# A recurrence whose filling work is handed out anew: one output projection and half of the last values go to the two last scans

## The chip, the cores and the metric

The kernel runs on one core of a Trainium2 chip. The metric is device microseconds (us) of one execution. The kernel before took 1845.09 us, the median of three runs (1844.77 to 1849.04). The profile shows one execution of 1847.34 us, whose span from first to last instruction is 1845.5 us.

## What is computed

Two layers of a diffusion transformer on 512 latent and 256 context tokens of width 1024, in fp32. Layer 0 mixes the tokens by attention, layer 1 by a gated linear recurrence in both directions (HGRN2, 8 heads of 128 key and 128 value channels). Each layer ends in a SwiGLU feed-forward block. Of layer 1 only the latent tokens are needed behind the mixer. The part that the change touches, cut from the reference:

```python
def hgrn2_mixer(h_lat, h_ctx, w_in, lb, out_norm, w_o, with_ctx_out):
    def gates(z):
        f = lb + (1.0 - lb) * jax.nn.sigmoid(z.astype(jnp.float32))
        return heads(jnp.log(f)), heads(1.0 - f)
    ...
    s_fw = hgrn2_final_state(kc_fw, gc_fw, vc)            # context tokens
    s_bw = hgrn2_final_state(flip(kc_bw), flip(gc_bw), flip(vc))
    q, gate = query_gate(h_lat)
    g_fw, k_fw, g_bw, k_bw, v = recurrent_inputs(h_lat)
    o_fw, _ = hgrn2_chunk_scan(q, k_fw, g_fw, v, s_fw)
    o_bw, _ = hgrn2_chunk_scan(flip(q), flip(k_bw), flip(g_bw), flip(v), s_bw)
    return readout(o_fw + flip(o_bw), gate), y_c          # rms_norm, sigmoid gate, @ w_o
```

and then `h = h + gt1 * y` and the feed-forward block.

## The kernel before

Activations lie with channels on the 128 partitions and tokens along the free axis. Each large fp32 product is three products of a high and a low part (`mm3`, lines 112 to 114): weights are loaded into a ring of 1024-column tiles (`load_split`: 4 raw buffers, 3 for the high and 3 for the low parts), ScalarE casts the high part (line 88) and VectorE subtracts it (line 91, "split").

The recurrence runs head by head. One head scan (`scan_head`) is a generator of 14 steps. First VectorE adds the two directions' keys (`kfb`) and TensorE forms the product `A` (line 1548). Then come seven levels: in each, TensorE forms a product `lv` of halves of the chunks (line 1566), ScalarE copies the keys for it (`kc`, 2 buffers), VectorE scales the queries (`QD`, line 1573) and copies `lv` into `A` under a mask (line 1581), and GpSimd scales the keys (`KD`, line 1573). Then the keys are transposed (`ktp`), the states are formed (`pu`, `S`) and the output is read out (`ho`). Behind the readout stands a chain over ScalarE (`osq`), VectorE (`oss`, `on`) and GpSimd (power, and the gating `on*sg`), whose result is transposed (`hot`) in the next scan and scaled into `oth` and `otl`. `kfb` and `osq` share one buffer, and so do the six-column factors `FB` of all heads.

A scan alone leaves TensorE waiting. So the projections are put between its steps as filling work (`Fill.run` with a credit for each step): `head_proj` (products `hq` of 512 columns and `hz` of 512 and 256: query and the two forget gates of a head), `pair_proj` (`hv`, 256 columns: values of two heads), `gate_proj` (`hg`, 256 columns: output gates of two heads) and `wo_pair` (`hwo`, 512 columns: output projection of two heads, with the residual on VectorE, line 676). `head_proj` ends each gate with `FB` and `KD` on GpSimd (lines 1514 and 1515), which the next head's first product needs. The scans 1 to 6 (h = 0 to 5) run one after the other, the two last ones interleaved. Each engine executes in the order in which this code issues. What a scan doesn't use of its fill is drained behind it; the last `wo_pair` goes into the feed-forward block.

Of the kernel before, what the change touches and what calls it, by code (L numbers as in the profile page):

```python
# [16 lines left out]
P = 128  # L17
D = 1024
# [24 lines left out]
TAIL_BUDGET = (8, 1.6)  # L43
# [4 lines left out]
def kernel(  # L48
# [212 lines left out]
    def sumsq_add(acc, sqp, h, k, first, eng=None, tag="sq", bufs=2, width=T):  # L261
        if first:
            ACT.activation(acc, h, AF.Square)
        else:
            sq = sqp.tile([P, width], F32, tag=tag, bufs=bufs, name=f"sq{k}")
            sq = sq[:, : h.shape[1]]
            ACT.activation(sq, h, AF.Square)
            (eng or DVE).tensor_tensor(acc, acc, sq, op=ALU.add)
# [391 lines left out]
    hT = [hpool.tile([P, T], F32, name=f"hT{k}") for k in range(KT)]  # L660

    def residual_in():
# [5 lines left out]
        for k in range(KT):  # L668
# [3 lines left out]
            ACT.copy(hT[k], ps[:, 0:T])  # L672
# [149 lines left out]
    def ffn(layer, only_lat, pre, begin, tail=None):  # L822
# [172 lines left out]
        def fo_out(p_, o, ps, v, a, e):  # L995
            residual(o, ps, layer, 5, v, a, e)
            if p_ == len(parts) - 1:
                sumsq_add(acc_n[:, a:e], late_pool[0], hT[o][:, a:e], o, o == 0, POOL if v else DVE,
                          tag=f"g{8 + (o + v) % 2}", bufs=1, width=n)
# [120 lines left out]
        for h in range(2):  # L1120
            hs = slice(h * H, (h + 1) * H)
            for o in range(KT):
                next(pre)
                sumsq_add(acc_n[:, hs], fp, hT[o][:, hs], o, o == 0, DVE if o % 2 else POOL, tag="sw", bufs=2, width=512)
# [82 lines left out]
    def ffn_plain(layer, only_lat, begin, late, pre=None, tail=None):  # L1207
# [33 lines left out]
        def token_scale():  # L1241
            acc_o = fp.tile([P, T], F32, tag="gl0", name="acc_o")
            for k in range(KT):
                odd = k % 2
                sumsq_add((acc_o if odd else acc_n)[:, :n], fp, hT[k][:, :n], k, k < 2, POOL if odd else DVE)
# [47 lines left out]
        for part, (j0, nj) in enumerate(PARTS[1]):  # L1293
# [50 lines left out]
            def fo_chain(o, w, ps, v, a, e):  # L1344
# [3 lines left out]
                if final:  # L1348
                    sumsq_add(acc_n[:, a:e], fp, hT[o][:, a:e], o, o == 0)
# [106 lines left out]
    def token_proj(c0, ntok, name, evac):  # L1456
        ws = [w_in(c0, 256, 4 * i, 4, f"{name}{i}") for i in range(2)]
        for t in range(ntok):
# [21 lines left out]
    def pair_proj(pr_):  # L1480
        v2 = hnp.tile([P, NT, 256], F32, tag=f"xt2{'hl'[pr_ % 2]}", name="v2")
        sg2 = hp.tile([P, NLT, 256], F32, tag="sg2", bufs=1, name="sg2")
        hv["v", pr_], hv["g", pr_] = v2, sg2
        yield from token_proj(4 * D + pr_ * 256, NT, f"hv{pr_}", lambda t, ps: ACT.copy(v2[:, t], ps))

    def gate_proj(pr_):
        sg2 = hv["g", pr_]
        yield from token_proj(D + pr_ * 256, NLT, f"hg{pr_}",
# [49 lines left out]
    def scan_head(h):  # L1538
# [98 lines left out]
        oth = hop.tile([P, NL], F32R, tag=f"oth{h % 2}", name="oth")  # L1637
        otl = hop.tile([P, NL], F32R, tag=f"otl{h % 2}", name="otl")
# [24 lines left out]
    for h in range(GH - 2):  # L1663
        fill = Fill()
        budget = 20.8
        if h % 2 == 0:
            fill.add(gate_proj(h // 2))
            budget += 10.4
            if h >= 2:
# [95 lines left out]
```

## Time and profile before

| | |
|---|---|
| median of three runs | 1845.09 us |
| profiled execution, its span | 1847.34 us, 1845.5 us |
| attention, first feed-forward block | to about 960 us of the span |
| recurrence (eight scans) | about 970 to 1453 us |
| second feed-forward block | about 1453 to 1845 us |
| TensorE, VectorE, ScalarE, GpSimd busy | 96%, 66%, 42%, 29% of the span |

Times in the rows are microseconds from the span's start. In a timeline a row begins with start and duration, then engine, line, operation, result and inputs; a bracket at the end gives the idle time of that engine just before and what ended it. A row may stand for several instructions (x8). The granted clock is a share of TensorE's full speed, 2.4 GHz.

### The profile page before, as it was taken

To read this page: it belongs to the slowest core of one execution; us is meant where nothing else is said; L and a number is where in the kernel's file an instruction comes from. 1 tells how busy PE (TensorE), PEld (TensorE's weight loads), DVE (VectorE), ACT (ScalarE), POOL (GpSimd) and SP (SyncE) were. 2 spreads that over 40 slices of the span, in tenths; PEclk is the share of its full clock that TensorE was granted. 3 is DMA by queue.
4 is the path that set the end of the run, shared out by engine and by line. 5 is a ranking of instruction groups with operands and counts; after the bars stand their busy time and mean duration, and the time that the engine had idled before them with its cause. 6 is when DMAs were issued, how large, how long until landed. Compare 5 with 4: busy or idle time off the path is not lost.

```text
span 1845.5 us, 30295 instructions
## 1 busy us (share of the span) xinstructions
PE 1780.8 (96%) x11929; PEld 1627.0 (88%) x11929; DVE 1224.5 (66%) x2097; ACT 765.9 (42%) x1465; POOL 543.2 (29%) x508
## 2 busy tenths in 40 slices
PE   8979999999999999999999989999998999999998
PEld 6779688988899989898988889898997899898997
DVE  3586688888878787878756475656738774344443
ACT  4333787777533425252545233333323432222234
POOL 1244255445513314141315264443535100000000
PEclk9999999999999999999999999999999999999999
DMA  9433510002033232525231212112211253333321
GB/s 329 160 115 86 166 59 24 14 11 75 23 111 112 71 119 75 154 87 171 63 109 45 69 58 81 59 57 80 80 52 29 86 166 92 93 89 94 100 85 56
DMA packets 213198, 166.41 MB, mean 90 GB/s; under 512 B 7696, under 2 KB 190144, under 8 KB 213056
## 3 DMA queue, kind: packets, MB, share of 16 engines
q1 hardware_dynamic: 212768, 163.43, 28.7%
q8 instruction: 94, 1.54, 0.3%
q10 hardware_dynamic: 288, 1.05, 0.1%
q14 instruction: 48, 0.39, 0.1%
HBM read 162.36 MB, written 2.10 MB: 89 GB/s over the span
## 4 chain that ended last, share of the span: by engine, by line
PE 83%; DVE 8%; ACT 3%; POOL 3%; issue 2%; DMA 1%; POOLq 0%; SPq 0%; DVEq 0%; ACTq 0%
PE ffo L112 5%; PE ffo L113 5%; PE ffo L114 5%; PE ffi L112 5%; PE ffi L113 5%; PE ffi L114 5%; PE pt L703 3%; PE x L112 2%; PE x L113 2%; PE x L114 2%; PE lv L1566 2%; PE hz L112 2%; PE hz L113 2%; PE hz L114 2%; PE sc L645 2%
## 5 line engine op out<-in xcount | busy, mean ns | idle before, releaser
L112 PE MATMUL ffi<-fnh,whi_fi 128*128 128x256 f32 x704 | 198.9, 283 | 0.1
L113 PE MATMUL ffi<-fnl,whi_fi 128*128 128x256 f32 x704 | 198.0, 281 | 0.9 <-DVE fnl L1236 0.9
L114 PE MATMUL ffi<-fnh,wlo_fi 128*128 128x256 f32 x704 | 197.8, 281 | 0.0
L113 PEld LDWEIGHTS ffi<-fnl,whi_fi 128*128 128x128 f32 x704 | 133.2, 189 | 1.5 <-DVE fnl L1236 1.3
L112 PEld LDWEIGHTS ffi<-fnh,whi_fi 128*128 128x128 f32 x704 | 132.7, 189 | 0.5 <-issue 0.3
L114 PEld LDWEIGHTS ffi<-fnh,wlo_fi 128*128 128x128 f32 x704 | 132.8, 189 | 0.0
L676 DVE SCALAR_TENSOR_TENSOR hT<-ffo,modc,hT 128x512 f32<-128x512 f32 (+1 forms) x106 | 67.0, 636 | 90.8 <-PE ffo L114 90.7
L1573 POOL TENSOR_TENSOR KD<-KD,tot 128x384 f32<-128x384 f32 x96 | 101.5, 1081 | 67.8 <-ACT kc L1556 66.2
L280 POOL TENSOR_TENSOR rc<-rc,mhalf 128x2 f32<-128x2 f32 (+2 forms) x7 | 6.3, 906 | 379.3 <-DVE rc L278 379.3
L693 POOL TENSOR_SCALAR pf<-pf,st 128x768 f32<-128x768 f32 (+1 forms) x96 | 73.6, 769 | 127.9 <-DVE st L692 91.6
L88 ACT CAST whi_fi<-raw_fi 128x1024 fp32r<-128x1024 f32 x44 | 46.2, 1051 | 146.7 <-PE ffi L113 72.7
L114 PE MATMUL ffo<-gh,wlo_w 128*128 128x512 f32 (+1 forms) x304 | 102.6, 338 | 0.0
L113 PE MATMUL ffo<-gl,whi_w 128*128 128x512 f32 (+1 forms) x304 | 102.3, 337 | 0.0
L112 PE MATMUL ffo<-gh,whi_w 128*128 128x512 f32 (+1 forms) x304 | 101.6, 337 | 0.0
L91 DVE TENSOR_TENSOR ptl<-pt,pth 128x384 fp32r<-128x384 f32 (+1 forms) x160 | 79.8, 523 | 12.4 <-ACT pth L88 11.2
L1556 ACT COPY kc<-KD 128x256 f32<-128x256 f32 x112 | 43.0, 414 | 102.7 <-PE lv L1566 37.6
L689 DVE TENSOR_REDUCE st<-sc 128x1 f32<-128x768 f32 (+1 forms) x96 | 74.2, 773 | 15.3 <-PE sc L646 12.5
L88 ACT CAST pth<-pt 128x384 fp32r<-128x384 f32 (+1 forms) x160 | 69.9, 461 | 34.2 <-PE pt L703 22.4
L235 DVE SCALAR_TENSOR_TENSOR adacc<-adw,csil,adacc 128x512 f32<-128x512 f32 x98 | 82.0, 850 | 2.1 <-DMA adw<-in_ada_w_dram 1.8
L1573 DVE TENSOR_TENSOR QD<-QD,tot 128x256 f32<-128x256 f32 x96 | 55.5, 619 | 41.1 <-PE lv L1566 40.4
L691 ACT ACTIVATE pf<-sc,st 128x768 f32<-128x768 f32 (+1 forms) x96 | 73.4, 765 | 19.3 <-DVE st L689 18.4
L703 PE MATMUL pt<-ident,pf 128*128 128x128 f32 x448 | 72.2, 276 | 5.1 <-DVE ptl L91 3.9
(852 smaller groups left out, 5980.6 us busy)
## 6 DMA issues: line engine op xcount, KB each, us to landing
raw_fi<-in_ffn_w_in_dram SPq DMA_DIRECT2D x44, 512.0 KB, 3.7
adw<-in_ada_w_dram SPq DMA_DIRECT2D x40, 512.0 KB, 4.5
adw<-in_ada_w_dram SPq DMA_DIRECT2D x80, 256.0 KB, 3.1
raw_hz<-in_hgrn_w_in_dram SPq DMA_DIRECT2D x14, 512.0 KB, 3.6
raw_fo<-in_ffn_w_out_dram SPq DMA_DIRECT2D x16, 448.0 KB, 3.8
adr<-in_ada_w_dram SPq DMA_DIRECT2D x16, 256.0 KB, 4.7
adr<-in_ada_w_dram SPq DMA_DIRECT2D x8, 512.0 KB, 6.8
raw_wq<-in_attn_w_qkv_dram SPq DMA_DIRECT2D x8, 512.0 KB, 6.2
```

The costliest lines, as they stand in the source:

```text
L88: ACT.copy(hi, src)
L91: (eng or DVE).tensor_tensor(lo, src, hi.bitcast(F32), op=ALU.subtract)
L112: PE.matmul(ps, ahi, bhi, start=first, stop=False, **kw)
L113: PE.matmul(ps, ahi, blo, start=False, stop=False, **kw)
L114: PE.matmul(ps, alo, bhi, start=False, stop=last, **kw)
L235: pin(DVE.scalar_tensor_tensor(a, raw, cc, a, op0=ALU.mult, op1=ALU.add))
L676: DVE.scalar_tensor_tensor(hT[o][:, a:e], ps, mcol(layer, ch, o, v), hT[o][:, a:e], op0=ALU.mult, op1=ALU.add)
L689: DVE.tensor_reduce(st3[:, 0:1], ps[:, :nk], op=ALU.max, axis=AX.X, negate=True)
L691: ACT.activation(pf, ps[:, :nk], AF.Exp, bias=st3[:, 0:1], accum_out=st3[:, 1:2])
L693: POOL.tensor_scalar(pf, pf, st3[:, 2:3], 1.0, op0=ALU.mult, op1=ALU.mult)
L703: PE.transpose(pt[:, i * P : (i + 1) * P], pf[:, (i0 + i) * P : (i0 + i + 1) * P], ident)
L1573: eng.tensor_tensor(view, view, f, op=ALU.mult)
```

## The change

- The fill of the first scan is `head_proj(1)` and then `gate_proj(0)`; it was the other way round.
- `wo_pair(1)` (48 products of 512 columns) leaves the fifth scan (h = 4), the second half of the tokens of `pair_proj(3)` (72 products of 256 columns) leaves the sixth (h = 5); both are filling work of the two last scans now. The halves of `pair_proj` load and split their weights each for itself. The credits of each step are set anew (`TAIL_BUDGET` 1.6 to 2.6).
- The context tokens lie in tiles of their own (`hC`), and two of these are used again for `oth` and `otl` of the heads 2 and 3, which now live longer. Where an operation spanned latent and context tokens, it is issued in two pieces (the copy in `residual_in`, the square in `sumsq_add`).

```diff
--- before.py
+++ after.py
@@ -40,7 +40,7 @@
 Q_LAG = 3
 SOFTMAX_LAG = 3
 PV_LAG = 6
-TAIL_BUDGET = (8, 1.6)
+TAIL_BUDGET = (8, 2.6)
 LEVELS = [1, 2, 4, 8, 16, 32, 64]
 
 
@@ -258,14 +258,14 @@
 
 
 
-    def sumsq_add(acc, sqp, h, k, first, eng=None, tag="sq", bufs=2, width=T):
-        if first:
-            ACT.activation(acc, h, AF.Square)
-        else:
-            sq = sqp.tile([P, width], F32, tag=tag, bufs=bufs, name=f"sq{k}")
-            sq = sq[:, : h.shape[1]]
-            ACT.activation(sq, h, AF.Square)
-            (eng or DVE).tensor_tensor(acc, acc, sq, op=ALU.add)
+    def sumsq_add(acc, sqp, hs, k, first, eng=None, tag="sq", bufs=2, width=T):
+        sq = acc if first else sqp.tile([P, width], F32, tag=tag, bufs=bufs, name=f"sq{k}")
+        at = 0
+        for h in hs:
+            ACT.activation(sq[:, at : at + h.shape[1]], h, AF.Square)
+            at += h.shape[1]
+        if not first:
+            (eng or DVE).tensor_tensor(acc, acc, sq[:, :at], op=ALU.add)
 
     def rstd_cols(pl, acc, n, tag="rc", late=False):
         nt = n // P
@@ -657,7 +657,18 @@
     qes.close()
 
     hpool = pool("hT", side="right")
-    hT = [hpool.tile([P, T], F32, name=f"hT{k}") for k in range(KT)]
+    class Tokens:
+        def __init__(self, lat, ctx_):
+            self.lat, self.ctx = lat, ctx_
+
+        def __getitem__(self, at):
+            a, e = at[1].start, at[1].stop
+            if e <= NL:
+                return self.lat[:, a:e]
+            return self.ctx[:, a - NL : e - NL]
+
+    hC = [hpool.tile([P, 2, NC], F32, tag=f"hC{k}", name=f"hC{k}") for k in range(KT // 2)]
+    hT = [Tokens(hpool.tile([P, NL], F32, name=f"hT{k}"), hC[k // 2][:, k % 2]) for k in range(KT)]
 
     def residual_in():
         for k in range(KT):
@@ -669,7 +680,8 @@
             ps = s2(f"rx{k}")
             for t in range(NT):
                 PE.transpose(ps[:, t * P : (t + 1) * P], hT[k][:, t * P : (t + 1) * P], ident)
-            ACT.copy(hT[k], ps[:, 0:T])
+            ACT.copy(hT[k][:, 0:NL], ps[:, 0:NL])
+            ACT.copy(hT[k][:, NL:T], ps[:, NL:T])
             yield
 
     def residual(o, ps, layer, ch, v, a, e):
...
@@ -1242,7 +1254,7 @@
             acc_o = fp.tile([P, T], F32, tag="gl0", name="acc_o")
             for k in range(KT):
                 odd = k % 2
-                sumsq_add((acc_o if odd else acc_n)[:, :n], fp, hT[k][:, :n], k, k < 2, POOL if odd else DVE)
+                sumsq_add((acc_o if odd else acc_n)[:, :n], fp, [hT[k][:, :n]], k, k < 2, POOL if odd else DVE)
             DVE.tensor_tensor(acc_n[:, :n], acc_n[:, :n], acc_o[:, :n], op=ALU.add)
             yield
             rc = rstd_cols(fp, acc_n[:, :n], n)
...
@@ -1453,9 +1465,9 @@
         src = hgrn_w_in[0, k0 * P : (k0 + nk) * P, c0 : c0 + n].rearrange("(k p) n -> p k n", p=P)
         return load_split(src, [P, nk, n], name, eng)
 
-    def token_proj(c0, ntok, name, evac):
+    def token_proj(c0, toks, name, evac):
         ws = [w_in(c0, 256, 4 * i, 4, f"{name}{i}") for i in range(2)]
-        for t in range(ntok):
+        for t in toks:
             ps = s2(name)
             ts_ = slice(t * P, (t + 1) * P)
             for k in range(KT):
@@ -1477,15 +1489,16 @@
 
     hv = {}
 
-    def pair_proj(pr_):
-        v2 = hnp.tile([P, NT, 256], F32, tag=f"xt2{'hl'[pr_ % 2]}", name="v2")
-        sg2 = hp.tile([P, NLT, 256], F32, tag="sg2", bufs=1, name="sg2")
-        hv["v", pr_], hv["g", pr_] = v2, sg2
-        yield from token_proj(4 * D + pr_ * 256, NT, f"hv{pr_}", lambda t, ps: ACT.copy(v2[:, t], ps))
+    def pair_proj(pr_, toks=range(NT)):
+        if toks.start == 0:
+            hv["v", pr_] = hnp.tile([P, NT, 256], F32, tag=f"xt2{'hl'[pr_ % 2]}", name="v2")
+            hv["g", pr_] = hp.tile([P, NLT, 256], F32, tag="sg2", bufs=1, name="sg2")
+        v2 = hv["v", pr_]
+        yield from token_proj(4 * D + pr_ * 256, toks, f"hv{pr_}{toks.start}", lambda t, ps: ACT.copy(v2[:, t], ps))
 
     def gate_proj(pr_):
         sg2 = hv["g", pr_]
-        yield from token_proj(D + pr_ * 256, NLT, f"hg{pr_}",
+        yield from token_proj(D + pr_ * 256, range(NLT), f"hg{pr_}",
                               lambda t, ps: ACT.activation(sg2[:, t], ps, AF.Sigmoid))
 
     def head_proj(h):
@@ -1634,8 +1647,11 @@
         for ck in range(NLT):
             PE.transpose(pt[:, ck * P : (ck + 1) * P], on[:, ck], ident)
         wcol = cols2[:, 32 + h : 33 + h]
-        oth = hop.tile([P, NL], F32R, tag=f"oth{h % 2}", name="oth")
-        otl = hop.tile([P, NL], F32R, tag=f"otl{h % 2}", name="otl")
+        if h in (2, 3):
+            oth, otl = (hpool.tile([P, NL], F32R, tag=f"hC{2 * (h - 2) + i}", name="oth" if i == 0 else "otl") for i in range(2))
+        else:
+            oth = hop.tile([P, NL], F32R, tag=f"oth{h % 2}", name="oth")
+            otl = hop.tile([P, NL], F32R, tag=f"otl{h % 2}", name="otl")
         ACT.activation(oth, pt, AF.Copy, scale=wcol)
         DVE.scalar_tensor_tensor(otl, pt, wcol, oth.bitcast(F32), op0=ALU.mult, op1=ALU.subtract)
         hv["o", h] = (oth, otl)
@@ -1663,16 +1679,16 @@
     for h in range(GH - 2):
         fill = Fill()
         budget = 20.8
+        if h == 0:
+            fill.add(head_proj(1))
         if h % 2 == 0:
             fill.add(gate_proj(h // 2))
-            budget += 10.4
-            if h >= 2:
-                budget += 10.4
+            budget += 20.8 if h == 2 else 10.4
         else:
             fill.add(head_proj(h + 1))
-            fill.add(pair_proj(h // 2 + 1))
-            budget += 15.6
-        if h % 2 == 0:
+            fill.add(pair_proj(h // 2 + 1, range(NT if h < GH - 3 else NT // 2)))
+            budget += 15.6 if h < GH - 3 else 7.8
+        if h % 2 == 0 and h:
             fill.add(head_proj(h + 1))
         cur = scan_head(h)
         for i in range(NSTEP - 2):
@@ -1684,8 +1700,8 @@
                 for _ in tail:
                     pass
                 tail = None
-                if h % 2 == 0:
-                    fill.add(wo_pair(h // 2 - 1))
+                if h == 2:
+                    fill.add(wo_pair(0))
         fill.drain()
         tail = cur
     afill.drain()
@@ -1699,7 +1715,9 @@
             for _ in tail:
                 pass
     fill.drain()
+    fill.add(pair_proj(GH // 2 - 1, range(NT // 2, NT)))
     fill.add(gate_proj(GH // 2 - 1))
+    fill.add(wo_pair(GH // 2 - 3))
     fill.add(wo_pair(GH // 2 - 2))
     next(sa)
     live = [sb, sa]
```

GpSimd, from the last key scalings of the first scan to those of the second: `FB` and `KD` (lines 1514 and 1515 before) are the second head's factors and keys, `oss` and `on` (lines 1624 to 1629) the first head's readout. Before:

```order
L1573 TENSOR_TENSOR KD_10747<-KD_10747,tot32_11163 128x12x32 x2
L1573 TENSOR_TENSOR KD_10747<-KD_10747,tot64_11197 128x6x64 x2
L1514 TENSOR_SCALAR FB_11148<-sgz_11269,lbt_5285 128x768
L1515 TENSOR_SCALAR KD_11149<-sgz_11269,lbt_5285 128x768
L1624 TENSOR_SCALAR oss_11358<-oss_11358 128x4
L1625 TENSOR_TENSOR oss_11358<-oss_11358,mhalf_73 128x4
L1629 TENSOR_TENSOR on_11362<-on_11362,sg2_10760 128x512
L1514 TENSOR_SCALAR FB_11148<-sgz_11377,lbt_5285 128x768
L1515 TENSOR_SCALAR KD_11149<-sgz_11377,lbt_5285 128x768
L1573 TENSOR_TENSOR KD_11149<-KD_11149,FB_11148 128x384 x2
```

Now (lines 1527 and 1528 for `FB` and `KD`, 1586 for the scalings, 1637 to 1642 for the readout):

```order
L1586 TENSOR_TENSOR KD_10767<-KD_10767,tot32_11146 128x12x32 x2
L1527 TENSOR_SCALAR FB_10992<-sgz_11110,lbt_5297 128x768
L1528 TENSOR_SCALAR KD_10993<-sgz_11110,lbt_5297 128x768
L1586 TENSOR_TENSOR KD_10767<-KD_10767,tot64_11173 128x6x64 x2
L1527 TENSOR_SCALAR FB_10992<-sgz_11215,lbt_5297 128x768
L1528 TENSOR_SCALAR KD_10993<-sgz_11215,lbt_5297 128x768
L1637 TENSOR_SCALAR oss_11395<-oss_11395 128x4
L1638 TENSOR_TENSOR oss_11395<-oss_11395,mhalf_73 128x4
L1586 TENSOR_TENSOR KD_10993<-KD_10993,FB_10992 128x384 x2
L1642 TENSOR_TENSOR on_11399<-on_11399,sg2_10780 128x512
```

The second `FB` and `KD` of the second head stood behind the first head's gating `on`; now both pairs stand ahead of the readout.

VectorE, in the sixth scan: `QD_13193` before and `QD_13228` now are the sixth head's queries, `wlo_hz60` and `wlo_hz61` the low parts of the weights for the two forget gates of the seventh head, `hv30` and `hv31` (now `hv300` and `hv301`) those for the last values. Before:

```order
L91 TENSOR_TENSOR wlo_hz60_13584<-raw_hz60_13582,whi_hz60_13583 128x1024
L235 SCALAR_TENSOR_TENSOR acc_n_5277<-adw1416_13229,csil_81,acc_n_5277 128x512
L91 TENSOR_TENSOR wlo_hz61_13699<-raw_hz61_13697,whi_hz61_13698 128x1024
L242 STREAM_TRANSPOSE adt1410_13715<-acc_n_5277 128x512
L243 TENSOR_REDUCE adpart14_11461<-adt1410_13715 128x16
L1573 TENSOR_TENSOR QD_13193<-QD_13193,FB_13191 128x256 x2
L1581 COPY_PREDICATED A_13523<-masks_10561,lv_13569 128x512
L91 TENSOR_TENSOR wlo_hv30_13793<-raw_hv30_13791,whi_hv30_13792 128x1024
L1573 TENSOR_TENSOR QD_13193<-QD_13193,tot2_13578 128x128x2 x2
L1581 COPY_PREDICATED A_13523<-masks_10561,lv_13604 128x512
```

Now:

```order
L1586 TENSOR_TENSOR QD_13228<-QD_13228,tot16_13608 128x16x16 x2
L1529 TENSOR_TENSOR QD_13524<-q_13520,FB_13522 128x512
L242 STREAM_TRANSPOSE adt1410_13640<-acc_n_5289 128x512
L1594 COPY_PREDICATED A_13467<-masks_10581,lv_13646 128x512
L243 TENSOR_REDUCE adpart14_11481<-adt1410_13640 128x16
L1586 TENSOR_TENSOR QD_13228<-QD_13228,tot32_13655 128x8x32 x2
L1594 COPY_PREDICATED A_13467<-masks_10581,lv_13680 128x512
L1586 TENSOR_TENSOR QD_13228<-QD_13228,tot64_13689 128x4x64 x2
L1594 COPY_PREDICATED A_13467<-masks_10581,lv_13707 128x512
L91 TENSOR_TENSOR wlo_hz61_13661<-raw_hz61_13659,whi_hz61_13660 128x1024
L91 TENSOR_TENSOR wlo_hv300_13770<-raw_hv300_13768,whi_hv300_13769 128x1024
```

The split for the second gate stood ahead of the first level; now it stands behind the last.

TensorE, in the sixth scan as well: `lv` is a level product, `ktp` the transposes behind the seventh. Before, at the sixth level:

```order
L113 MATMUL hz_13696<-hnb21l_10524,whi_hz61_13698 128x256
L114 MATMUL hz_13696<-hnb21h_10523,wlo_hz61_13699 128x256
L1566 MATMUL lv_13760<-QD_13193,kc_13757 128x128 x4
L112 MATMUL hz_13696<-hnt4h_10525,whi_hz61_13698 128x256
L113 MATMUL hz_13696<-hnt4l_10526,whi_hz61_13698 128x256
L114 MATMUL hz_13696<-hnt4h_10525,wlo_hz61_13699 128x256
```

Now, at the fifth, sixth and seventh:

```order
L114 MATMUL hz_13541<-hnb22h_10547,wlo_hz60_13544 128x256
L1579 MATMUL lv_13646<-QD_13228,kc_13643 128x128 x4
L1579 MATMUL lv_13680<-QD_13228,kc_13677 128x128 x4
L1579 MATMUL lv_13707<-QD_13228,kc_13704 128x128 x4
L1609 MATMUL ktp_13733<-ident_64,KD_13227 128x128 x4
L112 MATMUL hz_13658<-hnb11h_10541,whi_hz61_13660 128x512
L113 MATMUL hz_13658<-hnb11l_10542,whi_hz61_13660 128x512
```

Each level product was followed by projection work; now the three last ones and the transposes follow each other.

## Rows read from the trace of the kernel before

**Rows 1.** The page: busy time, share of the span and instructions of each engine.
```profile
PE 1780.8 (96%) x11929; PEld 1627.0 (88%) x11929; DVE 1224.5 (66%) x2097; ACT 765.9 (42%) x1465; POOL 543.2 (29%) x508
```

**Rows 2.** Stretches: length, busy us of PE PEld DVE ACT POOL, clock, DMA share, GB/s.
```profile
1070.00:1074.00 4.00, 3.63 (x13) 3.24 (x14) 3.90 (x5) 0.80 (x3) 3.60 (x3) 0.57 0.17 64
1250.00:1380.00 130.00, 128.95 (x841) 116.27 (x841) 76.36 (x119) 42.55 (x77) 52.01 (x45) 1.00 0.23 69
1384.00:1416.60 32.60, 27.01 (x201) 24.62 (x201) 30.67 (x47) 12.61 (x30) 23.20 (x22) 1.00 0.14 42
1416.60:1436.00 19.40, 18.32 (x124) 15.65 (x123) 11.52 (x25) 3.89 (x8) 2.50 (x3) 1.00 0.00 1
1436.00:1453.20 17.20, 15.07 (x60) 11.08 (x59) 13.53 (x20) 9.52 (x16) 2.56 (x4) 0.90 0.35 108
```

**Rows 3.** Timeline, join of first and second scan: start, duration, engine, instruction, [idle before].
```profile
1061.02 0.60 ACT L1621 ACTIVATE osq<-ho 128x512 f32<-128x512 f32 x1 [4.24 <-PE ho L1619]
1061.65 0.69 DVE L1623 TENSOR_REDUCE oss<-osq 128x4 f32<-128x512 f32 x1 [3.28 <-ACT osq L1621]
1062.33 1.05 ACT L88 CAST whi_hz<-raw_hz 128x1024 fp32r<-128x1024 f32 x1 [0.72 <-DVE oss L1623]
1062.71 1.01 POOL L1625 TENSOR_TENSOR oss<-oss,mhalf 128x4 f32<-128x4 f32 x1
1064.52 2.19 POOL L1629 TENSOR_TENSOR on<-on,sg 128x512 f32<-128x512 f32 x1 [0.80 <-DVE on L1627]
1066.36 0.39 PE L112 MATMUL hq<-hnb22h,whi_hq 128*128 128x512 f32 x1
1066.70 1.42 POOL L1514 TENSOR_SCALAR FB<-sgz,lbt 128x768 f32<-128x768 f32 x1
1068.11 1.49 POOL L1515 TENSOR_SCALAR KD<-sgz,lbt 128x768 f32<-128x768 f32 x1
...
1070.37 1.98 PE L1548 MATMUL lv<-q,kfb 128*128 128x128 f32 x8 [3.62 <-DVE kfb L1543]
...
1079.66 0.48 PE L1566 MATMUL lv<-QD,kc 128*128 128x128 f32 x2 [1.31 <-DVE QD L1573]
```

**Rows 4.** Timeline of TensorE, three stretches with products back to back.
```profile
1060.94 0.28 PE L113 MATMUL hz<-hnt4l,whi_hz 128*128 128x256 f32 x1
...
1062.13 0.28 PE L114 MATMUL hz<-hnb22h,wlo_hz 128*128 128x256 f32 x1
...
1253.03 1.06 PE L1566 MATMUL lv<-QD,kc 128*128 128x128 f32 x8
...
1446.18 0.40 PE L112 MATMUL hwo<-oth,whi_hwo 128*128 128x512 f32 x1
...
1452.95 0.40 PE L114 MATMUL hwo<-oth,wlo_hwo 128*128 128x512 f32 x1
```

**Rows 5.** Timeline of VectorE and GpSimd in the sixth scan.
```profile
1303.33 5.52 POOL L1573 TENSOR_TENSOR KD<-KD,tot 128x384 f32<-128x384 f32 x4
1303.84 2.05 DVE L91 TENSOR_TENSOR wlo_hz<-raw_hz,whi_hz 128x1024 fp32r<-128x1024 f32 x1
...
1309.66 1.20 DVE L91 TENSOR_TENSOR wlo_hv<-raw_hv,whi_hv 128x1024 fp32r<-128x1024 f32 x1
1310.79 1.44 DVE L1573 TENSOR_TENSOR QD<-QD,tot 128x256 f32<-128x256 f32 x2
1311.05 1.92 POOL L1573 TENSOR_TENSOR KD<-KD,tot 128x384 f32<-128x384 f32 x2 [2.21 <-ACT kc L1556]
1312.15 0.73 DVE L1581 COPY_PREDICATED A<-masks,lv 128x512 f32<-128x512 uint8 x1
...
1318.34 0.76 DVE L1573 TENSOR_TENSOR QD<-QD,tot 128x256 f32<-128x256 f32 x2 [1.19 <-PE lv L1566]
```

**Rows 6.** Timeline of VectorE in the two last scans, starts of two levels.
```profile
1388.84 1.62 DVE L1573 TENSOR_TENSOR QD<-QD,FB 128x256 f32<-128x256 f32 x2
...
1402.57 2.10 DVE L1573 TENSOR_TENSOR QD<-QD,tot 128x256 f32<-128x256 f32 x2
```

More of the change, by code (lines that the diff above doesn't have):

```diff
@@ L997, in fo_out @@
             if p_ == len(parts) - 1:
-                sumsq_add(acc_n[:, a:e], late_pool[0], hT[o][:, a:e], o, o == 0, POOL if v else DVE,
+                sumsq_add(acc_n[:, a:e], late_pool[0], [hT[o][:, a:e]], o, o == 0, POOL if v else DVE,
                           tag=f"g{8 + (o + v) % 2}", bufs=1, width=n)
@@ L1123, in ffn @@
                 next(pre)
-                sumsq_add(acc_n[:, hs], fp, hT[o][:, hs], o, o == 0, DVE if o % 2 else POOL, tag="sw", bufs=2, width=512)
+                sumsq_add(acc_n[:, hs], fp, [hT[o][:, a:e] for _, a, e in halves[h]], o, o == 0, DVE if o % 2 else POOL, tag="sw", bufs=2, width=512)
                 if h == 1 and o == 1:
@@ L1348, in fo_chain @@
                 if final:
-                    sumsq_add(acc_n[:, a:e], fp, hT[o][:, a:e], o, o == 0)
+                    sumsq_add(acc_n[:, a:e], fp, [hT[o][:, a:e]], o, o == 0)
                     if layer == 1:
```

## The prediction

> **What bounds the kernel now.** The page comes first: TensorE is busy 1780.8 us, 96% of the span, and no other engine is above 66% [rows 1]. So time is won only where TensorE waits, and moving its work helps only if the work goes from a stretch where TensorE is full into one where it is not. The second view is therefore the table of stretches, over the recurrence (eight head scans, about 970 to 1453 us), which the change alone touches. From 1250 to 1380, in the fifth and sixth scan, TensorE is busy 128.95 of 130 us: work taken out there shortens the time by its whole length. In the two last scans it is not full: 27.01 of 32.6 us up to 1416.6 (VectorE 30.67 and GpSimd 23.20 there), 18.32 of 19.4 up to 1436, 15.07 of 17.2 up to 1453.2 with a mean granted clock of 0.90 [rows 2]. The third view is the timeline at the join of first and second scan, where the longest wait of the recurrence stands: the A product of the second scan starts at 1070.37 after 3.62 us without work, and from 1070 to 1074 the granted clock is 0.57, half speed for nearly all of it [rows 2, 3].
>
> **Rates.** A 512-column product follows the last one by (1452.95 - 1446.18)/29 = 0.233 us, a 256-column one by (1062.13 - 1060.94)/10 = 0.119 [rows 4].
>
> **Part 1, work leaves the full scans.** The second output projection is 48 products of 512 columns, 48 x 0.233 = 11.2 us, and half of the last values is 72 of 256 columns, 72 x 0.119 = 8.6. Both stood where TensorE is full: -19.8 us there.
>
> **Part 2, the two last scans take it.** Three pieces.
> Up to 1416.6 the fill was 63 gate products of 256 columns and 14 of the third output projection, 63 x 0.119 + 14 x 0.233 = 10.8 us; now it is 72 value products and 63 of the gate, 135 x 0.119 = 16.1. That is 5.3 us more against 5.6 idle (32.6 - 27.0). If it fits wholly the cost is 0; if none fits, 5.3. On VectorE two splits and two residuals make room for three splits. A split of 1024 columns took 1.20 us at 1309.66, where GpSimd was idle, and 2.05 at 1303.84, beside four scalings of GpSimd; a scaling pair on VectorE took 0.76 alone at 1318.34 and 1.44 beside GpSimd at 1310.79 [rows 5]. So I price the three splits at 2.05, 6.2 us, and what they replace at two splits of 1.2 and two 512-column operations of 0.7, 3.8: VectorE gets 2.4 more with 1.9 free (32.6 - 30.7). Both engines end nearly full; I take +2.5, near the VectorE figure, with 0 and 5.3 + 3.6 = 8.9 (each product and each split in series) as ends.
> The Trainium skill (SBUF — State Buffer, "Who interferes with whom") states that a VectorE instruction with two inputs in SBUF and a GpSimd instruction that reads SBUF block each other through one shared read port, for the whole instruction. The trace agrees: 0.76 against 1.44, 1.20 against 2.05. By a reading without it the three splits would cost 3.6 instead of 6.2, this piece nothing, and the sum below would be -1.8.
> From 1416.6 to 1436 the output products rise from 32 to 48 (48 x 0.233 = 11.2, +3.7) with 1.1 us idle: +3.0.
> From 1436 the fill was 50 output products, 11.7 us, with 2.1 us of waits and 1.7 lost to the clock (0.10 x 17.2). Now 96 remain, 22.4 us. About 0.9 of the waits stays. A new one comes in front of the last 48: the scaled outputs of the last two heads stand on ScalarE behind a weight cast whose slot comes free with the last use of the fifth weight block, three products before the previous projection ends. It costs about the cast, 1.05, plus the output's copy, 0.60 as the square beside it, less 0.7 for three products and plus 0.4 of handing over [rows 3]: 1.4. So 24.7 instead of 17.2: +7.5, or +6 if that wait hides.
> Sum of parts 1 and 2: -19.8 + 2.5 + 3.0 + 7.5 = -6.8, ends -10.8 and -0.4.
>
> **Part 3, the first scan's order.** Before, the second scan's first product waits for a chain: square 1061.02, sum 1061.65, power 1062.71, gating 1064.52 (2.19), then FB 1066.70 (1.42) and KD 1068.11 (1.49), and only then the added keys and the product at 1070.37; the cover ends with the product at 1066.36 [rows 3]. Now the head's projection stands first in the fill, its FB and KD are issued ahead of the first scan's readout, and 10 of its products become cover: the keys need only square, sum and their own addition, some 2 us against 10 x 0.233 = 2.3. The 3.62 goes, so does the 1.31 behind it at 1079.66, and the clock's fall (4 us at 0.57: 1.7 lost). Of 6.6 I leave 0.5: -6.1, ends -5 and -7.
>
> **Part 4, the fifth and sixth scan, where the loss comes.** Without the output projection and half of the values the fill is short, and the same wait appears one head pair later. The chain at the join of the fifth and sixth scan is that of rows 3, 9.35 us from the square to the product (1061.02 to 1070.37), less 0.7 because FB now runs while VectorE scales the output: 8.65. The cover is 12 and 17 products, 1.4 + 4.0 = 5.4. Wait 3.25; before, this join lost 0.5. If the clock falls as at 1070 it takes 1.7 more.
> Then the sixth scan's last three level products stand in a row, without fill between, because the split of the second gate's weights is behind the sixth level on VectorE. Between two of them lie a copy into A (0.73, row 1312.15), a scaling pair (1.44) and the handing over: 2.2 to 2.6 less the product before it, which makes 1.75 of wait at the second. The third has also the next head's scaled queries, a transpose and a sum of 512 columns on VectorE in its way, each about 0.7 as the sum in rows 3: 3.3. The gate's first low product then waits for that split behind one more scaling pair and copy, 1.6, and the next scan 0.45. A level product itself takes about 1 (row 1253.03) [rows 3 to 5]. In all 3.25 + 1.75 + 3.3 + 1.6 + 0.45 = 10.3, and 2.7 for the clock falling at the join and again here: +13.0. Low end 8.0: a join wait of 2.5 and no fall of the clock; high end 16, all three scalings stretched to 2.
>
> **Small things.** Join of sixth and seventh scan +0.3; eight more Squares and eight more copies on ScalarE, 0.3 (0 to 16 x 0.60 / 2 = 4.8; ScalarE is at 42%, rows 1, and waits there for TensorE). Separate context tiles issue nothing more.
>
> **Sum.** -6.8 - 6.1 + 13.0 + 0.6 = +0.7 us on the profiled execution, 1847.34, which is 2.25 above the median 1845.09 of the runs shown. On the median: 1845.8, say 1846.
>
> **Rivals.**
> (a) Faster, 1838: the join waits 2.5 and the clock does not fall, so the gap in the sixth scan costs 8.0, and the two last scans swallow their first piece at no cost. Sum 0.7 - 5.0 - 2.5 = -6.8. For it: 5.6 us idle stand ready up to 1416.6 [rows 2]. Against: half a clock followed the only wait of this kind in the trace.
> (b) Slower, 1852: the two last scans do not take the work. Their level period is three periods from 1388.84 to 1402.57, 4.6 us [rows 6], set by VectorE and GpSimd in turn. If each fill product and each split stands in series, the first piece costs 8.9 instead of 2.5: sum +7.1, 1852.2. It decides from a period of 5.6 us: seven levels x 1.0 more make the time 0.3% longer. For it: VectorE at 94%, GpSimd 71% there. Against: products wait on neither.
> (c) The reordered fill doesn't do what it says: GpSimd's order changes, but the keys' addition still stands behind the gating, and the 3.6 us wait stays with its clock: +0.7 + 6.1 = +6.8, 1852. For it: the square and the keys' sum use one buffer. Against: GpSimd's order has FB and KD ahead of the readout.
>
> **Chances.** Forecast (within 0.3%, 5.5 us, which is about what a measurement of this kernel can tell from no change) 0.50, own range 1840 to 1851; (a) 0.30; (b) 0.17; (c) 0.03. Faster by over 0.3% 0.30, within 0.50, slower 0.20. The range for 8 in 10 goes from 1837, where (a) lies, to 1853.
>
> **What would show it.** In the changed profile: no wait for added keys near 1066 and a granted clock of 1.0 there; at the start of the sixth scan a wait of about 3.3 us for them; three level products without fill before its transposes, with 6 to 7 us idle; TensorE above 97% up to the end of the two last scans, and about 1.4 us idle ahead of the last 48 output products. I am wrong if the sixth scan loses under 8 or over 16 us, or if the level period of the two last scans passes 5.6.

## The result and the profile after

The changed kernel takes 1850.09 us, median of 12 runs (1847.94 to 1855.20), the kernel before 1846.84 in 12 runs beside it. The ratio is 1.0019, 95% interval 1.0012 to 1.0026: 3.5 us slower (3.25 between the two medians), small but clear of zero, and inside the 0.3% that were forecast as no change. The profiled execution took 1851.83 us, with a span of 1850.0.

The page's first part, busy time and share of each engine, for the changed kernel:

```profile
PE 1780.5 (96%) x11929; PEld 1628.2 (88%) x11929; DVE 1227.3 (66%) x2099; ACT 768.8 (42%) x1483; POOL 537.6 (29%) x508
```

TensorE works as long as before (1780.8 us, [rows 1]), so the 4.5 us of longer span are idle time or work at a slow clock, and these must be sought by place. For that I cut both traces at the same events: the first product of a scan (A1, A8: first and last head), the square of each readout (osq) and the first product of the feed-forward block.

| stretch | before, us | changed, us | difference |
|---|---|---|---|
| start to A1 | 1013.30 | 1010.33 | -2.97 |
| A1 to osq2 (first and second scan) | 107.10 | 102.41 | -4.69 |
| osq2 to osq4 | 114.57 | 114.55 | -0.02 |
| osq4 to osq5 (fifth scan) | 60.84 | 52.44 | -8.40 |
| osq5 to osq6 (sixth scan) | 54.57 | 63.57 | +9.00 |
| osq6 to A8 | 33.63 | 31.05 | -2.58 |
| A8 to osq7 (levels of the two last) | 40.98 | 46.55 | +5.57 |
| osq7 to osq8 | 11.12 | 12.52 | +1.40 |
| osq8 to feed-forward block | 17.07 | 24.28 | +7.21 |
| feed-forward block to the end | 392.32 | 392.30 | 0 |

The first join came out as the order promised. TensorE's timeline there, changed kernel:

```profile
1062.34 1.16 PE L1561 MATMUL lv<-q,kfb 128*128 128x128 f32 x8
...
1072.01 1.20 PE L1579 MATMUL lv<-QD,kc 128*128 128x128 f32 x8 [1.22 <-DVE QD L1586]
```

No wait stands ahead of the second scan's first product, where 3.62 us stood [rows 3]; 1.22 remain in place of 1.31 behind it.

The sixth scan is the place of the loss. TensorE's timeline, then VectorE's, changed kernel:

```profile
1287.64 1.16 PE L1561 MATMUL lv<-q,kfb 128*128 128x128 f32 x8 [2.64 <-DVE kfb L1556]
...
1294.74 2.04 PE L1579 MATMUL lv<-QD,kc 128*128 128x128 f32 x8 [3.01 <-DVE QD L1586]
...
1309.04 1.05 PE L1579 MATMUL lv<-QD,kc 128*128 128x128 f32 x8
1311.03 1.13 PE L1579 MATMUL lv<-QD,kc 128*128 128x128 f32 x8 [0.94 <-ACT kc L1569]
1315.51 2.04 PE L1579 MATMUL lv<-QD,kc 128*128 128x128 f32 x8 [3.35 <-DVE QD L1586]
1317.34 1.06 PE L1609 MATMUL ktp<-ident,KD 128*128 128x128 f32 x4
```

```profile
1287.51 5.71 DVE L1593 TENSOR_TENSOR tot<-tot 128x384 f32<-128x384 f32 x6
1293.13 1.46 DVE L1586 TENSOR_TENSOR QD<-QD,FB 128x256 f32<-128x256 f32 x2
...
1314.10 1.25 DVE L1586 TENSOR_TENSOR QD<-QD,tot 128x256 f32<-128x256 f32 x2
...
1318.88 1.22 DVE L91 TENSOR_TENSOR wlo_hz<-raw_hz,whi_hz 128x1024 fp32r<-128x1024 f32 x1
```

Two groups of waits are to be seen. At the join the keys' sum is late (2.64), and then the first scaling of the queries, behind six factor products that VectorE took first (3.01). Later three level products and the transposes follow each other bare (0.94 and 3.35); the split of the second gate's weights comes only at 1318.88. Behind each group a row lasts 2.04 us where 1.05 is usual. The table of stretches (columns as in [rows 2]) shows why, with the scan itself in the first row:

```profile
1279.73:1343.30 63.57, 53.24 (x335) 47.97 (x334) 38.30 (x61) 19.26 (x36) 25.25 (x23) 0.89 0.18 54
1294.80:1300.30 5.50, 5.50 (x17) 4.73 (x18) 2.47 (x5) 0.71 (x2) 1.78 (x2) 0.50 0.31 95
1315.50:1320.90 5.40, 5.39 (x23) 4.86 (x24) 3.81 (x6) 2.20 (x4) 0.00 (x0) 0.50 0.31 92
```

For 5.5 and 5.4 us the granted clock is 0.50, the lower level, so 2.75 + 2.7 = 5.45 us are lost beside the waits. In the same scan before, the clock was 1.00 and TensorE worked 54.30 of 54.57 us:

```profile
1295.81:1350.38 54.57, 54.30 (x384) 50.05 (x383) 35.16 (x54) 18.07 (x35) 25.24 (x21) 1.00 0.23 68
```

The two last scans, before and changed, from A8 on:

```profile
1384.01:1424.99 40.98, 35.40 (x258) 31.72 (x259) 35.11 (x57) 14.33 (x34) 23.20 (x22) 1.00 0.12 34
1436.11:1453.18 17.07, 14.94 (x58) 10.96 (x57) 13.51 (x20) 9.49 (x16) 2.56 (x4) 0.90 0.35 108
```

```profile
1374.35:1420.90 46.55, 42.52 (x323) 39.48 (x324) 35.98 (x58) 17.39 (x40) 24.00 (x22) 1.00 0.16 51
1433.42:1457.70 24.28, 23.49 (x104) 18.44 (x103) 19.78 (x29) 9.74 (x15) 3.02 (x4) 1.00 0.40 120
```

TensorE's idle time falls from 5.58 to 4.03 us up to osq7 and from 2.13 to 0.79 behind osq8. The one wait left behind osq8 is that ahead of the last 48 output products:

```profile
1446.23 0.96 PE L112 MATMUL hwo<-oth,whi_hwo 128*128 128x512 f32 x3 [0.79 <-ACT oth L1655]
```

The levels became longer. VectorE's scaling pairs of the last head, the last one before, then first, fourth and last of the changed kernel:

```profile
1416.82 0.76 DVE L1573 TENSOR_TENSOR QD<-QD,tot 128x256 f32<-128x256 f32 x2
```

```profile
1379.17 1.63 DVE L1586 TENSOR_TENSOR QD<-QD,FB 128x256 f32<-128x256 f32 x2
...
1396.69 2.06 DVE L1586 TENSOR_TENSOR QD<-QD,tot 128x256 f32<-128x256 f32 x2
...
1411.08 0.76 DVE L1586 TENSOR_TENSOR QD<-QD,tot 128x256 f32<-128x256 f32 x2
```

From 1379.17 to 1396.69 three periods took 5.84 us each, where they took 4.58 before [rows 6]; all six took 5.32 each, against 4.66 (1388.84 to 1416.82).

### The profile page after: what moved, and what is told of

Same layout as the page of the kernel before. It is cut to its first block, busy times and chain, and to the rows that moved or that the text cites. A ratio compares the mean times of both kernels' runs of the same rounds, so it can differ in the third digit from the quotient of the medians.

```text
span 1850.0 us, 30323 instructions
## 1 busy us (share of the span) xinstructions
PE 1780.5 (96%) x11929; PEld 1628.2 (88%) x11929; DVE 1227.3 (66%) x2099; ACT 768.8 (42%) x1483; POOL 537.6 (29%) x508
## 3 DMA queue, kind: packets, MB, share of 16 engines
q10 hardware_dynamic: 288, 1.05, 0.1%
## 4 chain that ended last, share of the span: by engine, by line
PE 81%; DVE 9%; ACT 4%; POOL 4%; issue 2%; DMA 0%; SPq 0%; POOLq 0%; DVEq 0%; ACTq 0%
PE ffo L112 5%; PE ffo L113 5%; PE ffo L114 5%; PE ffi L112 4%; PE ffi L113 4%; PE ffi L114 4%; PE pt L715 2%; PE x L112 2%; PE x L114 2%; PE x L113 2%; PE lv L1579 2%; PE hz L112 2%; PE hz L113 2%; PE hz L114 2%; DVE QD L1586 1%
## 5 line engine op out<-in xcount | busy, mean ns | idle before, releaser
L688 DVE SCALAR_TENSOR_TENSOR hT<-ffo,modc,hT 128x512 f32<-128x512 f32 (+1 forms) x66 | 48.3, 733 | 87.0 <-PE ffo L114 87.0
L1579 PE MATMUL lv<-QD,kc 128*128 128x128 f32 x448 | 65.6, 292 | 15.0 <-DVE QD L1586 9.9
```

What stands on the lines that cost most here:

```text
L688: DVE.scalar_tensor_tensor(hT[o][:, a:e], ps, mcol(layer, ch, o, v), hT[o][:, a:e], op0=ALU.mult, op1=ALU.add)
L1579: PE.matmul(ps[:, cs], kc[:, cs], mv, start=True, stop=True)
```

## The experiments

The first theory was that the loss lies in the sixth scan and has two separate causes: the join is late because the output projection left the fifth scan, and the last levels lie bare because half of the values left. The rival was that the two last scans take none of the work moved there. Each run was timed beside the kernel before on its chip; a ratio is to that, with a 95% interval.

**The first scan's order alone** (h0). The kernel before with

```diff
+        if h == 0:
+            fill.add(head_proj(1))
         if h % 2 == 0:
             fill.add(gate_proj(h // 2))
...
-        if h % 2 == 0:
+        if h % 2 == 0 and h:
             fill.add(head_proj(h + 1))
```

> The kernel before with the new order of the first scan's fill alone. Theory 1 (the loss lies in the sixth scan): the second scan's wait of 3.62 us, the 1.31 behind it and the slow clock go, and nothing later gives it back. In the changed kernel the readout of the second scan came 4.7 us earlier against the start of the first scan, so 4.7 us faster, ratio 0.9975. Rival (the two last scans give it all back): here nothing is moved there, so the same 0.9975. A third view, that the gain at the join only moves a wait to a later join, gives 1.000, with a wait of 2 us or more at a later join.

Measured: 0.9972 (0.9961 to 0.9983), 1841.71 us. From A1 to osq2 it took 101.63 us, 5.47 less than before, and nothing later gave it back, so the third view is out; the theory and the rival expected the same here. This part alone makes the kernel 5 us faster, and the rest of the change costs 0.47%, 8.7 us.

**The output projection moved, the values not** (wo_only). The changed kernel with

```diff
-            fill.add(pair_proj(h // 2 + 1, range(NT if h < GH - 3 else NT // 2)))
-            budget += 15.6 if h < GH - 3 else 7.8
+            fill.add(pair_proj(h // 2 + 1, range(NT)))
+            budget += 15.6
...
-    fill.add(pair_proj(GH // 2 - 1, range(NT // 2, NT)))
```

> The changed kernel, but all of the last values stay in the sixth scan; so the first scan's order and the moved output projection remain. Theory 1 (two causes in the sixth scan: its first product waits because the output projection left the fifth scan, some 8 to 9.5 us with the clock; the three last levels lie bare because half of the values left, some 8 us): -4.7 for the first scan, -11.2 moved, +9.5 at the join, +5.6 in the two last scans (11.2 less the 5.6 that they took in the changed kernel) = -0.8, ratio 0.9996; three last levels with fill between. Rival (the two last scans take nothing): -4.7 - 11.2 + 11.2 and no loss in the sixth scan = -4.7, ratio 0.9975.

Measured: 0.9995 (0.9986 to 1.0005). The rival's 0.9975 lies outside. TensorE's timeline has the two waits at the join and none in the last levels:

```profile
1289.03 1.16 PE L1561 MATMUL lv<-q,kfb 128*128 128x128 f32 x8 [3.41 <-DVE kfb L1556]
...
1298.35 2.05 PE L1579 MATMUL lv<-QD,kc 128*128 128x128 f32 x8 [2.70 <-DVE QD L1586]
```

and the clock falls behind them (stretches):

```profile
1298.40:1303.80 5.40, 5.40 (x17) 4.63 (x18) 1.85 (x4) 0.71 (x2) 1.78 (x2) 0.50 0.16 48
```

**The values moved, the output projection not** (hv_only).

```diff
-            budget += 20.8 if h == 2 else 10.4
+            budget += 20.8 if h else 10.4
...
-                if h == 2:
-                    fill.add(wo_pair(0))
+                if h in (2, 4):
+                    fill.add(wo_pair(h // 2 - 1))
...
-    fill.add(wo_pair(GH // 2 - 3))
```

> The changed kernel, but the second output projection stays in the fifth scan; the first scan's order and the moved half of the values remain. Theory 1: -4.7 - 8.6 + 8.1 for the three bare levels (0.94 + 3.35 + 0.39 of waits and 3.4 of slow clock in the changed kernel) + 3.0 in the two last scans = -2.2, ratio 0.9988; no wait for the added keys at the start of the sixth scan, but a wait of about 3.3 us ahead of its last level product. Rival (the two last scans take nothing): -4.7 - 8.6 + 8.6 = -4.7, ratio 0.9975.

Measured: 0.9994 (0.9986 to 1.0003); 0.9988 is inside, the rival's 0.9975 is not. The waits are in the last levels and none at the join:

```profile
1312.65 1.13 PE L1579 MATMUL lv<-QD,kc 128*128 128x128 f32 x8 [0.94 <-ACT kc L1569]
1317.12 2.04 PE L1579 MATMUL lv<-QD,kc 128*128 128x128 f32 x8 [3.34 <-DVE QD L1586]
```

So each of the two moves costs some 0.22% on top of the first scan's order, and together they cost 0.47%: they add up. Each is a move together with its cut of the credits: the fifth scan's went from 41.6 to 31.2 with the output projection, the sixth's from 36.4 to 28.6 with the values. The next run and the last one part the two for the values; no run does for the output projection.

**The sixth scan's credits restored** (bud). One number of the changed kernel:

```diff
-            budget += 15.6 if h < GH - 3 else 7.8
+            budget += 15.6
```

> The changed kernel with one number restored: the credits that the sixth scan's fill gets per scan stay at 36.4 instead of 28.6. The work moved is the same. Theory 1: the second gate's weights are reached earlier, fill stands between the three last levels again, and the 3.35 and 0.94 us of waits and the slow clock behind them go: 8.1 us less than the changed kernel, ratio 0.9975 against before; the wait at the join of some 2.6 us stays. Rival (the sixth scan's gap is only slack that the two last scans would otherwise wait for): the gap closes and the time stays at 1.002, with more idle time in the two last scans.

Measured: 0.9991 (0.9982 to 1.0000), 0.28% or 5.2 us less than the changed kernel; 8.1 were expected. The bare levels are gone, the waits at the join are longer than expected, and the clock stays at 1.00 through the whole scan (TensorE's timeline, then the scan):

```profile
1291.85 1.16 PE L1561 MATMUL lv<-q,kfb 128*128 128x128 f32 x8 [3.41 <-DVE kfb L1556]
...
1301.17 1.20 PE L1579 MATMUL lv<-QD,kc 128*128 128x128 f32 x8 [2.71 <-DVE QD L1586]
```

```profile
1282.94:1341.30 58.36, 52.24 (x355) 46.97 (x354) 37.68 (x60) 19.09 (x36) 27.71 (x23) 1.00 0.24 72
```

This shows that the bare levels come from the number of credits, not from the work that left: the work is the same in both kernels. The size of 8.1 was too large for the runs. In the two profiled executions the time from osq5 to A8 fell by more, from 94.62 to 85.15 us; part of that is the slow clock at the join, which the execution of bud did not have.

**The projection first in the fifth scan too** (h4first).

```diff
-        if h == 0:
-            fill.add(head_proj(1))
+        if h in (0, 4):
+            fill.add(head_proj(h + 1))
...
-        if h % 2 == 0 and h:
+        if h == 2:
```

> The changed kernel with the fifth scan's fill in the order of the first one's: the projection of the next head first, then the gates. Nothing else. Theory 1 (the join and the three bare levels are two separate losses of the sixth scan): the wait for the added keys (2.64 us) and the 3.01 behind it go with their slow clock (1294.7 to 1300.4 at about 0.57, 2.5 us), -8.1 against the changed kernel, ratio 0.9975 against before; the 3.35 us wait ahead of the last level product stays. Rival (one loss: when the join is early, the bare levels wait longer, since the same chain over VectorE and GpSimd sets the end of the scan): ratio 1.001 to 1.002.

Measured: 1.0016 (1.0007 to 1.0025). The first theory fell here. The wait at the join did go, but the fifth scan got a new one at its second level. VectorE's timeline there, then TensorE's:

```profile
1231.46 1.59 DVE L91 TENSOR_TENSOR wlo_hz<-raw_hz,whi_hz 128x1024 fp32r<-128x1024 f32 x1
1232.97 1.67 DVE L235 SCALAR_TENSOR_TENSOR acc_n<-adw,csil,acc_n 128x512 f32<-128x512 f32 x1
1235.82 2.05 DVE L91 TENSOR_TENSOR wlo_hz<-raw_hz,whi_hz 128x1024 fp32r<-128x1024 f32 x1 [1.18 <-ACT whi_hz L88]
1237.79 1.51 DVE L235 SCALAR_TENSOR_TENSOR acc_n<-adw,csil,acc_n 128x512 f32<-128x512 f32 x1
1240.88 1.23 DVE L91 TENSOR_TENSOR wlo_hg<-raw_hg,whi_hg 128x1024 fp32r<-128x1024 f32 x1 [1.58 <-ACT whi_hg L88]
1242.02 2.17 DVE L1586 TENSOR_TENSOR QD<-QD,FB 128x256 f32<-128x256 f32 x2
```

```profile
1244.34 2.05 PE L1579 MATMUL lv<-QD,kc 128*128 128x128 f32 x8 [3.25 <-DVE QD L1586]
```

Three splits of weights for the new fill and two sums of another task stand on VectorE ahead of the first scaling, together with VectorE's own waits for ScalarE's casts (1.18 and 1.58). TensorE waits 3.25 us for the scaling, with the slow clock behind. Two of the splits lie beside GpSimd's work and take 1.59 and 2.05 instead of 1.23 us. So the place of the wait at the join is not the whole cause. A likely reading is that the fifth scan without the output projection has too little fill to cover VectorE wherever it is late. This is argued, not shown: the fifth scan's credits were cut with the projection, and no run gave them back.

**Both remedies** (h4bud), the two edits above together.

> The changed kernel with both remedies: the projection first in the fifth scan's fill and the sixth scan's credits left at 36.4. Theory 1: neither wait at the join (3.41 and 2.71 us in the run with the credits alone) nor bare levels. That run's ratio 0.9991 less 6.1 us: 0.9958, faster than the new order of the first scan alone (0.9972). Rival (the two last scans take nothing of what is moved): not faster than the new order of the first scan alone, 0.9972.

Measured: 0.9982 (0.9973 to 0.9991), neither 0.9958 nor better than the order alone. In its profile the stretch from osq4 to A8 took 137.82 us against 149.06 with the order alone: of the 19.8 us taken out, 11.2 were saved. From A8 to the feed-forward block it took 83.40 against 67.89, 15.5 more: the two last scans took 4.3 of 19.8. With the credits alone (bud) the stretch from osq4 to A8 had been 137.56: between these two executions the fifth scan's new order added nothing.

**Output projection moved, values in place, projection first in the fifth scan** (wo_h4): the edits of wo_only and h4first.

> The output projection moved, all values left in the sixth scan, and the projection first in the fifth scan's fill. Theory 1: the run with the output projection alone (0.9995) less its waits at the join, 3.41 + 2.70 us, and 3.2 of slow clock (1296 to 1304 at 0.60): -9.3, ratio 0.9945. Rival (the two last scans take nothing): 0.9972, as with the first scan's order alone.

Measured: 0.9995 (0.9986 to 1.0003), as wo_only without the remedy; 0.9945 missed, and so did the rival's 0.9972. The fifth scan has a new wait here too, 3.31 us at its second level.

**Both remedies and 3.6 credits in the two last scans** (h4bud36).

```diff
-TAIL_BUDGET = (8, 2.6)
+TAIL_BUDGET = (8, 3.6)
```

> Both remedies, and the credits of each step of the two last scans at 3.6 instead of 2.6, so that 48 instead of 96 output products stand behind their last transposes or close to them. If the two last scans still have room in their levels (0.92 + 0.96 + 0.65 + 0.81 + 0.51 us of waits in the changed kernel): 2 us less than with both remedies alone, ratio 0.9947. If each product put there delays VectorE's chain by as much as it saves behind it: the same, 0.9958. If the levels get longer than the work saved: above 0.9965.

Measured: 0.9971 (0.9960 to 0.9982), less than with 2.6 by 0.11%, though the intervals overlap, and no better than the order alone. From A8 on it took 80.66 us, so the levels do take some more: 7.0 of 19.8.

**Factor products in program order** (after_pin, h0_pin).

```diff
-            DVE.tensor_tensor(nt, t2[:, :, :, 0], t2[:, :, :, 1], op=ALU.mult)
+            pin(DVE.tensor_tensor(nt, t2[:, :, :, 0], t2[:, :, :, 1], op=ALU.mult))
```

> The changed kernel with the factor products (tot, line 1593) kept in program order on VectorE, so that the six of them that took 5.71 us from 1287.51 stand no longer ahead of the first query scaling of the sixth scan (1293.13). Theory: the 3.01 us wait at 1294.74 is theirs; it goes, and the slow clock behind it (2.5 us): 3 to 5.5 us less than the changed kernel, ratio 0.999 to 1.0003 against before. Rival: the wait is set by the scaling of keys on GpSimd (4.01 us from 1290.30), not by the six products: unchanged, 1.0019.

Measured: 1.0010 (1.0001 to 1.0019). The scaling now stands ahead of the factors on VectorE, and the wait of 3.01 us is gone:

```profile
1294.16 0.77 DVE L1586 TENSOR_TENSOR QD<-QD,FB 128x256 f32<-128x256 f32 x2 [2.77 <-PE lv L1579]
1294.84 0.95 DVE L1593 TENSOR_TENSOR tot<-FB 128x768 f32<-128x768 f32 x1
```

Of the expected 3 to 5.5 us the runs show 1.7, within the uncertainty of both. That the six factors made this wait is shown; what it is worth is not settled. In the profile the stretch from osq4 to A8 got 6.9 us shorter (140.16 against 147.06) and that from A8 to the feed-forward block 2.4 longer (85.76 against 83.35): the same edit seems to cost in the two last scans, which the next run tries by itself.

> The kernel before with the first scan's new order and the factor products in program order. In the scans that run one at a time no wait in front of a second level is left but 0.42 us, so there is little to win there; in the two last scans the factor products then stand inside each level's chain on VectorE. If they fitted into its gaps before and don't now: 1 to 3 us slower than 0.9972; if the order is all the same there: 0.9972.

Measured: 0.9995 (0.9987 to 1.0004), 0.23% or 4.2 us slower than the order alone, more than the 1 to 3 expected. From A8 to osq7 it took 48.25 instead of 40.98 us: in the two last scans the factor products fitted into VectorE's gaps before, and do better there.

**More credits in the two last scans, nothing moved** (h0t22): the order alone with `TAIL_BUDGET = (8, 2.2)`.

> The kernel before with the first scan's new order and 2.2 instead of 1.6 credits for each step of the two last scans; no work is moved between scans. If the levels of the two last scans have room for TensorE work (5.6 us without work up to the end of the levels), some 20 products go there and come out of the end: 2 us less than 0.9972, ratio 0.996. If each product there delays the chain over VectorE and GpSimd by its own time: 0.9972.

Measured: 0.9999 (0.9990 to 1.0008), slower than the order alone by 0.27%; 0.996 and 0.9972 were both missed. Up to osq7, 14 more output products than with 1.6 credits (39 against 25) cost only 0.31 us (41.29 against 40.98), so the levels have that room. But the work then lacks behind them, where states are formed:

```profile
1430.01 2.48 PE L1606 MATMUL pu<-v,KtT 128*128 128x128 f32 x10 [4.07 <-DVE S L1611]
1433.66 0.76 PE L1617 MATMUL ho<-v,A 128*128 128x128 f32 x2 [1.17 <-DVE S L1611]
```

4.07 and 1.17 us of waits, and a slow clock: from osq7 to osq8 17.07 instead of 11.13 us. Here the room in the levels was of no use to the work that was already behind them.

**The version that the runs point to** (hvbud): the first scan's order, half of the values moved, 36.4 credits in the sixth scan, the output projection left in place; the edits of hv_only and bud together.

> The new order of the first scan, half of the last values moved to the two last scans, the sixth scan's credits left at 36.4, and the output projection left in the fifth scan; so none of the two causes of loss, and the work moved is 8.6 us. Theory (a scan can give away work as long as its fill still reaches all of its levels, and the two last scans take some of it): against the run with the first scan's order alone the sixth scan and what follows up to the last head's first product get 8.6 us shorter (88.2 us there from the square of the fifth scan on), the two last scans 6.0 longer (73.9 against 67.9 us from that product to the feed-forward block, as with the values alone): -2.6, ratio 0.9958 to before. Rival (each product that leaves costs its time again, in the levels that it covered or where it goes): 0.9972 as with the order alone, or slower.

Measured: 1839.10 us, ratio 0.9961 (0.9948 to 0.9975), expected 0.9958. It beats the kernel before and the changed one. In the sixth scan no wait above 0.25 us is left, and the stretch from A8 to the feed-forward block takes 73.91 us, as expected:

```profile
1300.89 1.20 PE L1579 MATMUL lv<-QD,kc 128*128 128x128 f32 x8 [0.25 <-DVE QD L1586]
...
1427.79 0.96 PE L112 MATMUL hwo<-oth,whi_hwo 128*128 128x512 f32 x3 [0.83 <-ACT oth L1655]
```

Its interval overlaps that of the order alone (0.9961 to 0.9983), so that the moved values add to it is likely but not settled, and the rival's 0.9972 is not excluded. From hv_only it differs by the sixth scan's credits alone, and these are worth 0.33%, 6.1 us. With its credits kept, the move of the values no longer costs anything: of the 8.6 us taken out, 7.8 stayed away from osq4 to A8 (141.22 against 149.06), and the two last scans got 6.0 longer.

## Why the prediction was right

The forecast was no change, because two gains and one loss of like size were read from the trace; all three are there, in the places named. Their sizes are another matter: each of the three parts came out slower than forecast, and two of the prediction's own signs of being wrong came true, the second in part. Step by step:

- Part 1, work that leaves: -19.8 us was the right amount. Fifth and sixth scan up to A8 became only 2.0 shorter (-8.40 + 9.00 - 2.58), so 17.8 were lost there.
- Part 4, this loss, was forecast at 13.0, at most 16. With 17.8, 16.1 of them in the sixth scan, it passed the first sign ("under 8 or over 16"). The waits of the sixth scan add up to 2.64 + 3.01 + 0.94 + 3.35 + 0.39 = 10.3, as forecast, but by luck. I had 1.75 us at the second bare level, which took 0.94, and 1.6 for the split, of which nothing came; instead the join had a second wait of 3.01 for the factor products, which I did not see. The term that was mis-sized is the clock: I took 2.7 for two falls, and they cost 5.45, since the second lasted as long as the first. The fifth scan lost about 1.4 more, of which 0.90 and 0.27 were new waits of its levels.
- Part 2, the two last scans: 14.2 us (5.57 + 1.40 + 7.21) against 13.0. Cut as the forecast cut it, at the last level product (1415.73 before, 1409.99 now) and at osq8, it is 3.9, 3.1 and 7.2 against 2.5, 3.0 and 7.5. The wait ahead of the last projection was 0.79 instead of 1.4. TensorE was busy 91% up to osq7, not above 97%. Rival (b) came in part: its sign, a level period of 5.6 us, was passed by the first three (5.84), but not by all six (5.32), and the first piece cost 3.9, not its 8.9.
- Part 3, the first scan: -4.7 in the profile and 5 us alone in the runs, against -6.1; 1.22 us of wait stayed where I left 0.5. Rival (c) did not come: the 3.62 us are gone.
- Small things: too small to be told apart here.
- Not forecast: the profiled execution of the changed kernel began its recurrence 2.97 us earlier. Other kernels with the same code up to there began it between 1010.5 and 1016.9, so this is the difference of single executions, not of the change.

Sum: -2.0 + 14.2 - 4.7 - 3.0 = +4.5 in the profiles; the runs say +3.5, the forecast was +0.7. The three parts erred by 4.8, 1.2 and 1.4 us, all to the slow side, and in the profile the early start hid 3.0 of that. So the mechanism was right, the range held, and the nearness of the number is in part luck. Rival (a) needed a clock that does not fall, and it fell twice. The step that I had not priced at all is the one that decides what to do with this change: part of the sixth scan's loss of 16.1 us (it was to get 7.1 shorter and got 9.0 longer) comes from a number, the credits, and not from the work that was moved. By the runs it is 5.2 us (bud against the changed kernel) or 6.1 (hvbud against hv_only).

What stays open: why h4first was no faster than the changed kernel. Its profiled execution was 3.8 us faster, with 4.3 us less in fifth and sixth scan together; the medians of the runs show none of it. The odd one may be the changed kernel's execution: from A1 to the end it took 839.7 us, 7.5 more than before, where the runs say 3.5. For every other kernel here these two figures agree within 2.1 us. So some 4 us of the losses sized above may belong to that one execution; whether the slow clock makes the difference is not shown.

## What to carry to other kernels

A stretch in which TensorE is 99% busy is not bound by TensorE alone when its work is filling: a product taken out can uncover the engine that it hid, and here 17.8 of 19.8 us came back as waits and slow clock. When the fill of a stage is cut, keep its rate, so that the weights for the last steps are loaded and split early enough, and let it run out where nothing waits. In the sixth scan this was worth 5 to 6 us; for the fifth it was not tried. And order fill by who needs its result: the next stage's first operands before what is needed late (5 us in the first scan; in the fifth, without the output projection, it gained nothing).

## What was not expected of the hardware

- The same pair of waits at the join was followed by a slow clock in one kernel and not in another: 3.41 and 2.70 us with a granted clock of 0.50 from 1298.4 to 1303.8 (wo_only), 3.41 and 2.71 us with 1.00 through the whole scan (bud).
- Where the clock fell it stayed at the lower level for 5.4 to 5.5 us in the changed kernel, although TensorE was busy all that time.
- VectorE's scaling pair took 0.76 us alone [rows 5] and 1.46 and 2.17 beside GpSimd's scalings (changed kernel at 1293.13, h4first at 1242.02), and a split 1.23 against 2.05. The Trainium skill (SBUF — State Buffer, "Who interferes with whom") states that a VectorE instruction with two SBUF inputs contends with a GpSimd instruction that reads SBUF; the traces agree.
